# A hybrid decoder trunk: ten taps of the last depthwise-conv tile on GpSimd instead of TensorE

## The chip, the cores and the metric

The kernel runs on one core of one Trainium2 chip. The metric is device time in microseconds of one execution. Before the change the median of three runs is 987.44 us (986.02 to 987.93). A core has TensorE (PE, matrix products into PSUM; its weight loads are shown as PEld), VectorE (DVE), ScalarE (ACT), GpSimd (POOL) and SyncE (SP, which issues the DMAs). Each works through its own queue in order and waits on semaphores for the others.

## The reference

A trunk of two layers on 512 tokens of 1024 channels, in float32. The part that the change touches is in layer 0: a projection of the normed input gives, among others, the two halves of a gated unit of 512 channels. The gated result goes through a causal depthwise convolution of 31 taps, a LayerNorm over channels and a swish. Beside it runs a multi-head latent attention of 8 heads. Both results are joined and projected.

```
proj = h @ w_in
a, g = proj[..., :CONV_CH], proj[..., CONV_CH:c0]
u = a * jax.nn.sigmoid(g)
u = causal_dwconv(u, conv_w, conv_b)              # 31 taps, each channel by itself
u = jax.nn.silu(layernorm(u, conv_ln_g, conv_ln_b))
o = mla_attention(qn, qr, kn, kr, v)              # 8 heads, 128-query blocks, softmax
return jnp.concatenate([u, o], axis=-1) @ w_out
```

Then come a gated MLP with a 3-tap convolution (2816 wide), a pooling mixer and a second MLP in layer 1, and a final norm.

## The kernel before

Channels lie on the 128 partitions and the 512 tokens along the free dimension. Every projection is done as three products of rounded halves (`mm3`, L107 to L110: high by high, high by low, low by high), for which ScalarE rounds each weight tile (`split`, L97) and VectorE subtracts the rounded part from the raw one (L98; both of its inputs are in SBUF). `split_scaled` (L102, L103) does the same to activations with a factor per channel. SyncE streams the weights through three buffers.

The first RMSNorm: ScalarE squares the input tiles (L224), GpSimd adds the squares (L226), TensorE sums over channels (L239), VectorE forms the reciprocal root (L205 to L212), TensorE spreads it over rows (L261) and ScalarE copies it (L265). The gated unit (`glu`, L430 to L438) multiplies with these rows.

The convolution works on four tiles of 128 channels. For tiles 0 to 2, ScalarE opens an accumulator in PSUM, the bank `conv`, with the last tap and the bias (L382). VectorE then adds 30 taps, one `scalar_tensor_tensor` on 128x512 each (L399: `u` shifted by j, times the weight column, plus the accumulator), and ScalarE copies the accumulator to an SBUF tile `side` (L414). There is one bank `conv`, so a tile must be closed before the next one is opened. Tile 3 is different: its first ten taps are matrix products. For each, GpSimd scales the identity by the tap's weights (L391, 128x128) and TensorE multiplies that diagonal with the shifted `u` (L392) into another bank, `aux`. VectorE adds taps 10 to 30 to it, and ScalarE closes it with the bias.

The taps are background work. `conv` puts VectorE's taps of all tiles in one list, and `pump` emits a few of them at fixed places: three after each projection of a latent, three after each projection of a gated unit, and two after each of the four query blocks of a head (`BLK`). GpSimd's and TensorE's share of tile 3 is a second list, emitted on every other query block (`i % 2`). What is left is emitted after the last head. The framework then orders each engine's queue at build time by priority and by its own estimate of when operands are ready. Its order may differ from that of the source: taps of tile 3 that the source emits after all heads run among them.

Per head, TensorE makes the scores (L523), VectorE adds the mask and takes the maximum (L526: scores in PSUM, mask in SBUF), then forms the product of maximum and scale for two blocks at once (L533, 128x2, both inputs in SBUF). ScalarE takes the exponential (L537) and, after VectorE's reciprocal (L542), divides (L544). TensorE transposes (L558), ScalarE copies (L560), TensorE multiplies with the values (L571), and VectorE scales the queries of a later head (L512: PSUM and SBUF).

After the heads, TensorE transposes the four `side` tiles (L643), VectorE takes the LayerNorm statistics (L645, L646, then the root), VectorE and ScalarE normalize (L663, L669), TensorE transposes back (L680) and ScalarE applies the swish (L682). Between these TensorE works on the attention's share of the output projection; the convolution's share follows.

Of the kernel before, what the change touches and what calls it, by code (L numbers as in the profile page):

```python
# [8 lines left out]
F32 = mybir.dt.float32  # L9
F32R = mybir.dt.float32r  # L10
I32 = mybir.dt.int32
AF = mybir.ActivationFunctionType
ALU = mybir.AluOpType
AX = mybir.AxisListType

P = 128
S = 512
# [5 lines left out]
CW = 31  # L23
# [9 lines left out]
C_NE, C_CB, C_LG, C_LB, C_QG, C_KG, C_NO, C_PS, C_NF, C_FN = 0, 8, 12, 16, 20, 23, 25, 33, 41, 57  # L33
# [3 lines left out]
N_COL = C_FB + 2 * NF  # L37

WARM = 40
PE_TAPS = 10  # L40
W_PAD, T_PAD, R_PAD = 48, 16, 120
GLU, LAT, BLK, END = 3, 4, 2, 0

# [2 lines left out]
def kernel(  # L46
# [20 lines left out]
    act, dve, pool, pe = nc.scalar, nc.vector, nc.gpsimd, nc.tensor  # L67
# [11 lines left out]
    def uid(s):  # L79
        count[0] += 1  # L80
        return f"{s}{count[0]}"

    def bank():
        return p_ps.tile([P, S], F32, tag="ps", name=uid("ps"))

    def aux(tag="aux"):
        return p_ps.tile([P, S], F32, tag=tag, bufs=1, name=uid(tag))

    def temp():
        return p_t.tile([P, 2 + S], F32, tag="t", name=uid("t"))[:, :S]  # L90

    def small(n=4, dt=F32):
        return p_s.tile([P, 8], dt, tag=f"s{dt}", name=uid("s"))[:, :n]
# [70 lines left out]
    def weights(ahead=1):  # L164
        given[0] += 1
        while len(ready) < min(given[0] + ahead, len(stream)):
            prepare()
        w = ready[given[0] - 1]
        ready[given[0] - 1] = None
        return w  # L170
# [18 lines left out]
    def c(i):  # L189
        return col[:, i : i + 1]  # L190

    sq = p_c.tile([P, 3, P], F32, name="sq")
    ident, ones, fold_kr = sq[:, 0, :], sq[:, 1, :], sq[:, 2, :]
# [80 lines left out]
    p_m = tc.alloc_tile_pool(name="mixer", bufs=1, side="left", reuse_waits="tile")  # L274
# [79 lines left out]
    for k in range(KD):  # L354
        w = weights(2)
# [13 lines left out]

    u, ys, work, pe_work = [], [], [], []

    def conv(m):
        cw = C_CW + CW * m
        side = p_m.tile([P, S], F32, tag="side", bufs=4, name=uid("side"))
        ys.append(side)
        st = {}

        def open_acc():  # L380
            st["acc"] = aux("conv")
            act.activation(  # L382
                st["acc"], u[m][:, CW - 1 : CW - 1 + S], AF.Identity,
                bias=c(C_CB + m), scale=c(cw + CW - 1),
            )

        def pe_tap(j):
            if j == 0:
                st["acc"] = aux()
            d = p_m.tile([P, P], F32, tag="tapped", bufs=4, name=uid("tap"))  # L390
            pool.tensor_scalar(d, ident, c(cw + j), None, op0=ALU.mult)  # L391
            pe.matmul(st["acc"], d, u[m][:, j : j + S], start=j == 0, stop=j == PE_TAPS - 1)  # L392

        def tap(j):
            while m == 3 and pe_work:
                pe_work.pop(0)()
            if not st:
                open_acc()
            i = dve.scalar_tensor_tensor(  # L399
                st["acc"], u[m][:, j : j + S], c(cw + j), st["acc"],  # L400
                op0=ALU.mult, op1=ALU.add,
            )
            if held:
                tc.add_manual_dep(
                    i.ins, held.pop().ins.name,
                    mybir.DependencyInfo(
                        mybir.DependencyClass.NoSync, mybir.DependencyReason.DATA
                    ),
                    reason="background",
                )  # L410

        def close():
            bias = c(C_CB + m) if m == 3 else 0.0
            act.activation(side, st["acc"], AF.Identity, bias=bias, scale=1.0)  # L414

        n_pe = PE_TAPS if m == 3 else 0
        pe_work.extend((lambda j=j: pe_tap(j)) for j in range(n_pe))
        work.extend((lambda j=j: tap(j)) for j in range(n_pe, CW if m == 3 else CW - 1))
        work.append(close)

    def pump(nd, np_=0):
        for _ in range(min(np_, len(pe_work))):
            pe_work.pop(0)()
        for _ in range(min(nd, len(work))):
            work.pop(0)()


    def glu(ps_a, ps_g):
        t = temp()
        dve.tensor_tensor(t, ps_g, rows0, op=ALU.mult)  # L430
        s = temp()
        act.activation(s, t, AF.Sigmoid)
        if len(u) == 3:
            act.activation(spare, s[:, 0:1], AF.Exp)
        dve.tensor_tensor(s, s, rows0, op=ALU.mult)
        ut = p_m.tile([P, 640], F32, tag="u", bufs=4, name=uid("u"))[:, : CW - 1 + S]
        pool.memset(ut[:, : CW - 1], 0.0)
        dve.tensor_tensor(ut[:, CW - 1 :], ps_a, s, op=ALU.mult)  # L438
        u.append(ut)
        conv(len(u) - 1)  # L440
# [6 lines left out]
    def latent(n, gain, width):  # L447
        parts, stat = [], Squares(width, dve)
        for m in range(n):
            ps = project()  # L450
            parts.append(s4())
            split_scaled(pair(parts[m]), ps, c(gain + m))
            stat.add(ps)
            pump(LAT)
        return parts, stat
# [5 lines left out]
    for m in range(2):  # L461
        kv_ps.append(project())
        stat_kv.add(kv_ps[m])
        pump(LAT)
# [10 lines left out]
    for m in range(2):  # L475
        t = temp()
# [5 lines left out]
    for _ in range(2):  # L482
        ps_a = project()
        pump(GLU)
        ps_g = project()
        glu(ps_a, ps_g)
        pump(GLU)
# [27 lines left out]
    def scores(h):  # L515
        q, key = qs.pop(h), keys[h // 2 % 2][:, h % 2, :]
        pb = p_a.tile([P, 1280], F32, tag="prob", bufs=3, name=uid("prob"))
        mx, nb, ls = small(), small(), small()
        blocks, at = [], 0
        for i in range(4):  # L520
            w = (i + 1) * P
            ps = bank()
            pe.matmul(ps[:, :w], q[:, i * P : (i + 1) * P], key[:, :w], start=True, stop=True)  # L523
            p = pb[:, at : at + w]
            at += w
            dve.tensor_tensor_reduce(  # L526
                out=p, in0=ps[:, :w], in1=causal[:, S - w :], scale=1.0,
                scalar=-3.0e38, op0=ALU.add, op1=ALU.max, accum_out=mx[:, i : i + 1],
            )
            blocks.append(p)  # L530
            if i % 2:
                two = slice(i - 1, i + 1)
                dve.scalar_tensor_tensor(  # L533
                    nb[:, two], mx[:, two], -1.0, q_scale[:, two], op0=ALU.mult, op1=ALU.mult
                )
                for n in (i - 1, i):
                    act.activation(  # L537
                        blocks[n], blocks[n], AF.Exp, bias=nb[:, n : n + 1],
                        scale=q_scale[:, n : n + 1], accum_out=ls[:, n : n + 1],
                    )  # L540
            pump(BLK, i % 2)
        dve.reciprocal(ls, ls)  # L542
        for i in range(4):
            act.activation(blocks[i], blocks[i], AF.Copy, scale=ls[:, i : i + 1])  # L544
        probs[h] = blocks
        sums[h] = ls[:, 3:4]
# [56 lines left out]
    for h in range(HEADS):  # L603
        scores(h)
        if h % 2 == 0 and h + 2 < HEADS:
            keys_of(h // 2 + 1)
        if h >= 1:
            transposes(h - 1)
        if h + 2 < HEADS:
            queries(h + 2)  # L610
        if h >= 3 and h % 2:
            values(h - 3)
            values(h - 2)
        pump(END)
# [25 lines left out]
    for i in range(4):  # L640
# [3 lines left out]
        st = p_s.tile([P, 6], F32, tag="bn", bufs=2, name=uid("bn"))  # L644
# [12 lines left out]
    with tc.high_priority():  # L657
# [4 lines left out]
        for i in range(2):  # L662
            dve.tensor_scalar(  # L663
                yts[i], yts[i], mv[:, i, 0:1], r_ln[:, i : i + 1],
                op0=ALU.subtract, op1=ALU.mult,
# [9 lines left out]
    for m in range(4):  # L675
# [5 lines left out]
        t = temp()  # L681
# [181 lines left out]
    for h in range(2):  # L863
        w = weights()
        for i in range(4):
# [11 lines left out]
            if (h, i) >= (0, 2):  # L877
                while zps:
                    i, ps = zps.pop(0)
# [151 lines left out]
```

## Time and profile before

| | |
|---|---|
| median of three runs | 987.44 us |
| the profiled execution | 985.52 us |
| its span, first to last instruction | 983.8 us |
| mean granted TensorE clock | 0.995 |
| attention and conv taps together | about 101.7 to 183.5 us |
| L399, taps, bank `conv` | 90, 751 ns mean |
| L399, taps, bank `aux` | 21, 751 ns mean |
| L391, GpSimd's scaled diagonals | 10, 809 ns mean |

All times of instructions are from one profiled execution. A row of instructions has start, length, engine, line, operation, output, inputs and shapes, and a count where neighbours are merged; idle time before it and what ended that stand in square brackets. A row of a group has its count, total busy time and mean length. A row of waits has who waited for whom, the total in us, how often, and the longest. In the chain of waits, every piece of time is put down to the work that the next step needed. Neighbours on one engine overlap a little, since the next one starts while the last one drains, so distances between starts are often shorter than lengths.

### The profile page before, as it was taken

The page shows a single profiled execution, that of the slowest core. Times are in us where ns is not written, and L with a number is a line of the kernel's source. Part 1 is how long each engine was busy: PE and PEld are TensorE (multiplying, and loading weights), DVE is VectorE, ACT ScalarE, POOL GpSimd, SP SyncE. Part 2 cuts the span into 40 slices and gives each one's busy share as a digit, 9 for nine tenths or more (in the row PEclk, how much of TensorE's full clock was granted, in tenths as well). Part 3 has the DMA queues.
Part 4 walks back from the last instruction along what each step waited for, and adds up shares of the span by engine and source line. Part 5 has one row for each costly group of instructions (what it writes and reads, how often), then busy time and mean ns, then how long its engine had stood idle before and what let it go on. Part 6 is the DMA issues. An engine that isn't in the chain of part 4 may idle for free.

```text
span 983.8 us, 11537 instructions
## 1 busy us (share of the span) xinstructions
PE 966.6 (98%) x4464; PEld 795.2 (81%) x4464; DVE 582.5 (59%) x910; ACT 403.4 (41%) x590; POOL 70.4 (7%) x105
## 2 busy tenths in 40 slices
PE   8999999999999999999999999999999999999996
PEld 6888765788888888888888889888888888888886
DVE  5999989863765556565333348485656555532323
ACT  6435788362443433343222246253333334332321
POOL 6001100031000000000000103100000000000111
PEclk9999999999999999999999999999999999999998
DMA  6332110222232232223232341322222222323212
GB/s 231 118 123 81 39 43 1 87 86 88 80 111 93 100 105 89 98 94 108 86 107 86 107 139 44 108 91 103 88 105 101 93 93 101 104 89 107 86 43 86
DMA packets 29478, 91.99 MB, mean 94 GB/s; under 512 B 4080, under 2 KB 6384, under 8 KB 29424
## 3 DMA queue, kind: packets, MB, share of 16 engines
q1 hardware_dynamic: 28880, 90.74, 27.1%
q8 instruction: 35, 0.57, 0.2%
q10 hardware_dynamic: 544, 0.52, 0.2%
q14 instruction: 19, 0.16, 0.0%
HBM read 89.02 MB, written 2.23 MB: 93 GB/s over the span
## 4 chain that ended last, share of the span: by engine, by line
PE 95%; DVE 2%; DMA 1%; ACT 1%; SPq 0%; issue 0%; DVEq 0%
PE ps L108 29%; PE ps L109 29%; PE ps L110 29%; PE ps L571 2%; PE ps L523 1%; PE aux L392 1%; PE aux L239 1%; PE ps L558 1%; PE aux L261 1%; DMA col<-in_cols_dram 0%; DMA x<-in_xT_dram 0%; DVE conv L399 0%; PE ps L900 0%; PE ps L899 0%; ACT hi L97 0%
## 5 line engine op out<-in xcount | busy, mean ns | idle before, releaser
L97 ACT CAST hi<-raw 128x1024 fp32r<-128x1024 f32 (+2 forms) x166 | 169.9, 1025 | 372.1 <-PE ps L109 335.3
L108 PE MATMUL ps<-xgh,hi 128*128 128x512 f32 x816 | 319.2, 391 | 2.8 <-ACT hi L97 2.8
L109 PE MATMUL ps<-xgl,hi 128*128 128x512 f32 x816 | 317.9, 390 | 0.0
L110 PE MATMUL ps<-xgh,lo 128*128 128x512 f32 x816 | 317.3, 390 | 0.0
L98 DVE TENSOR_TENSOR lo<-raw,hi 128x1024 fp32r<-128x1024 f32 (+2 forms) x166 | 200.8, 1211 | 160.2 <-ACT hi L97 159.8
L108 PEld LDWEIGHTS ps<-xgh,hi 128*128 128x128 f32 x816 | 153.3, 188 | 35.0 <-ACT hi L97 3.8
L110 PEld LDWEIGHTS ps<-xgh,lo 128*128 128x128 f32 x816 | 153.1, 188 | 32.4 <-DVE lo L98 0.5
L109 PEld LDWEIGHTS ps<-xgl,hi 128*128 128x128 f32 x816 | 153.3, 188 | 31.3
L108 PE MATMUL ps<-gh,hi 128*128 128x512 f32 (+1 forms) x374 | 141.2, 378 | 0.0
L109 PE MATMUL ps<-gl,hi 128*128 128x512 f32 (+1 forms) x374 | 141.1, 377 | 0.0
L110 PE MATMUL ps<-gh,lo 128*128 128x512 f32 (+1 forms) x374 | 141.0, 377 | 0.0
L108 PEld LDWEIGHTS ps<-gh,hi 128*128 128x128 f32 x374 | 70.4, 188 | 12.9
L109 PEld LDWEIGHTS ps<-gl,hi 128*128 128x128 f32 x374 | 70.4, 188 | 12.9
L110 PEld LDWEIGHTS ps<-gh,lo 128*128 128x128 f32 x374 | 70.4, 188 | 12.9
L728 DVE TENSOR_TENSOR t<-ps,rows 128x512 f32<-128x512 f32 x44 | 30.4, 691 | 77.2 <-PE ps L110 77.2
L226 POOL TENSOR_TENSOR sqr<-sqr,sqr 128x512 f32<-128x512 f32 x33 | 50.2, 1521 | 311.9 <-ACT sqr L224 282.0
L740 DVE TENSOR_TENSOR t<-ps,rows 128x512 f32<-128x512 f32 x44 | 30.4, 691 | 67.0 <-PE ps L110 66.8
L399 DVE SCALAR_TENSOR_TENSOR conv<-u,col,conv 128x512 f32<-128x512 f32 x90 | 67.6, 751 | 1.0 <-ACT conv L382 0.5
L735 DVE SCALAR_TENSOR_TENSOR t<-t,col,t 128x512 f32<-128x512 f32 x88 | 65.7, 749 | 1.4
L738 ACT ACTIVATE t<-t 128x512 f32<-128x512 f32 x44 | 27.8, 631 | 74.7 <-DVE t L735 74.7
L108 PE MATMUL ps<-s,hi 128*128 128x512 f32 x96 | 39.4, 419 | 0.0
L727 POOL MEMSET t<- 128x2 f32 x44 | 4.2, 99 | 491.1 <-DVE t L741 350.3
(187 smaller groups left out, 832.4 us busy)
## 6 DMA issues: line engine op xcount, KB each, us to landing
raw<-in_w_up_dram SPq DMA_DIRECT2D x88, 512.0 KB, 3.2
raw<-in_w_down_dram SPq DMA_DIRECT2D x44, 512.0 KB, 3.2
raw<-in_w_in_dram SPq DMA_DIRECT2D x10, 512.0 KB, 3.2
raw<-in_w_out_dram SPq DMA_DIRECT2D x8, 512.0 KB, 3.2
x<-in_xT_dram SPq DMA_DIRECT2D x8, 256.0 KB, 4.1
raw<-in_w_in_dram SPq DMA_DIRECT2D x8, 256.0 KB, 3.7
raw<-in_w_uq_dram SPq DMA_DIRECT2D x4, 384.0 KB, 3.0
raw<-in_w_ukv_dram SPq DMA_DIRECT2D x2, 512.0 KB, 4.1
```

The lines of the kernel that those rows point to most:

```text
L97: i = act.copy(dst[0], src)
L98: dve.tensor_tensor(dst[1], src, dst[0].bitcast(F32), op=ALU.subtract)
L108: pe.matmul(ps, a[0], b[0], start=start, stop=False)
L109: pe.matmul(ps, a[0], b[1], start=False, stop=False)
L110: pe.matmul(ps, a[1], b[0], start=False, stop=stop)
L226: self.engine.tensor_tensor(self.parts[0], self.parts[0], t, op=ALU.add)
L399: i = dve.scalar_tensor_tensor(st["acc"], u[m][:, j : j + S], c(cw + j), st["acc"], op0=ALU.mult, op1=ALU.add,)
L571: pe.matmul(ps[:, j * P :], vals[j][:, e, hp * P : (hp + 1) * P], pt, start=e == 0 and j == 0, stop=e == 1 and j == 3,)
L728: dve.tensor_tensor(ut[:, 2 : 2 + S], pu, rows, op=ALU.mult)
L735: dve.scalar_tensor_tensor(a, ut[:, j : j + S], c(fw + j * NF + f), a, op0=ALU.mult, op1=ALU.add)
L738: act.activation(a, a, AF.Silu)
L740: dve.tensor_tensor(b, pv, rows, op=ALU.mult)
```

## The change

The ten products of tile 3 on TensorE, and the ten scaled diagonals, go. Instead GpSimd computes taps 0 to 9 itself: a multiplication of the shifted `u` by the weight column, broadcast along the tokens, into a tile (for tap 0 into `side` itself), and for taps 1 to 9 an addition into `side`, 19 instructions on 128x512. Tile 3 now opens in the bank `conv` like the others, with the last tap and the bias on ScalarE, and VectorE adds taps 10 to 29. The close of tile 3 is an addition on VectorE of the accumulator and `side`, instead of ScalarE's copy. The temporary tiles become two of 128x512 instead of four of 128x128. GpSimd's list is emitted one tap per query block instead of one per two.

```diff
-PE_TAPS = 10
+POOL_TAPS = (0, 0, 0, 10)
...
-        def pe_tap(j):
-            if j == 0:
-                st["acc"] = aux()
-            d = p_m.tile([P, P], F32, tag="tapped", bufs=4, name=uid("tap"))
-            pool.tensor_scalar(d, ident, c(cw + j), None, op0=ALU.mult)
-            pe.matmul(st["acc"], d, u[m][:, j : j + S], start=j == 0, stop=j == PE_TAPS - 1)
+        def pool_tap(j):
+            t = side
+            if j:
+                t = p_m.tile([P, S], F32, tag="tapped", bufs=2, name=uid("tapped"))
+            w = c(cw + j).to_broadcast([P, S])
+            pool.tensor_tensor(t, u[m][:, j : j + S], w, op=ALU.mult)
+            if j:
+                pool.tensor_tensor(side, side, t, op=ALU.add)
 
         def tap(j):
-            while m == 3 and pe_work:
-                pe_work.pop(0)()
             if not st:
                 open_acc()
...
         def close():
-            bias = c(C_CB + m) if m == 3 else 0.0
-            act.activation(side, st["acc"], AF.Identity, bias=bias, scale=1.0)
-
-        n_pe = PE_TAPS if m == 3 else 0
-        pe_work.extend((lambda j=j: pe_tap(j)) for j in range(n_pe))
-        work.extend((lambda j=j: tap(j)) for j in range(n_pe, CW if m == 3 else CW - 1))
+            if n_pool:
+                dve.tensor_tensor(side, st["acc"], side, op=ALU.add)
+            else:
+                act.copy(side, st["acc"])
+
+        n_pool = POOL_TAPS[m]
+        pool_work.extend((lambda j=j: pool_tap(j)) for j in range(n_pool))
+        work.extend((lambda j=j: tap(j)) for j in range(n_pool, CW - 1))
         work.append(close)
...
-            pump(BLK, i % 2)
+            pump(BLK, 1)
```

More of the change, by code (lines that the diff above doesn't have):

```diff
@@ L368, in project @@
         return ps
-    u, ys, work, pe_work = [], [], [], []
+    u, ys, work, pool_work = [], [], [], []
     def conv(m):
@@ L412, in close @@
         def close():
-            bias = c(C_CB + m) if m == 3 else 0.0
-            act.activation(side, st["acc"], AF.Identity, bias=bias, scale=1.0)
-        n_pe = PE_TAPS if m == 3 else 0
-        pe_work.extend((lambda j=j: pe_tap(j)) for j in range(n_pe))
-        work.extend((lambda j=j: tap(j)) for j in range(n_pe, CW if m == 3 else CW - 1))
+            if n_pool:
[5 more added lines that the diff above has]
+        work.extend((lambda j=j: tap(j)) for j in range(n_pool, CW - 1))
         work.append(close)
     def pump(nd, np_=0):
-        for _ in range(min(np_, len(pe_work))):
-            pe_work.pop(0)()
+        for _ in range(min(np_, len(pool_work))):
+            pool_work.pop(0)()
         for _ in range(min(nd, len(work))):
```

## The prediction

> **What bounds the kernel now.** I read the busy totals and the chain of waits of the page first, then the stretches of time around the changed tile, then who waited for whom there, and last the single instructions on VectorE (DVE), GpSimd (POOL), ScalarE (ACT) and TensorE (PE).
>
> ```profile
> PE 966.6 (98%) x4464; PEld 795.2 (81%) x4464; DVE 582.5 (59%) x910; ACT 403.4 (41%) x590; POOL 70.4 (7%) x105
> PE 95%; DVE 2%; DMA 1%; ACT 1%; SPq 0%; issue 0%; DVEq 0%
> ```
>
> Over the whole span TensorE is the bound, and work taken from its queue seems to be worth its full length. That average hides the stage that the change touches. The columns below are stretch, length, then busy time and instructions of PE, PEld, DVE, ACT and POOL, the granted clock and the DMA.
>
> ```profile
> core 0: us, PE busy (x) PEld busy (x) DVE busy (x) ACT busy (x) POOL busy (x), PEclk, DMA share, GB/s
> 88.00:101.70 13.70, 13.70 (x60) 10.97 (x59) 11.43 (x16) 10.50 (x19) 0.14 (x1) 1.00 0.28 96
> 101.70:141.50 39.80, 39.80 (x165) 26.96 (x164) 35.83 (x91) 30.61 (x74) 4.33 (x6) 1.00 0.12 41
> 141.50:183.50 42.00, 39.54 (x179) 27.78 (x178) 40.66 (x86) 29.02 (x69) 0.00 (x0) 1.00 0.08 26
> 183.50:195.00 11.50, 9.91 (x50) 7.51 (x49) 9.35 (x27) 6.06 (x9) 0.00 (x0) 1.00 0.27 91
> ```
>
> From 101.7 to 183.5 us (attention, with the conv taps between) VectorE is busy 35.83 + 40.66 = 76.5 of 81.8 us. Only 5.3 us are idle, most of it for these reasons:
>
> ```profile
> DVE q L512 <- PE ps L110: 2.5, 3, 2.0
> DVE prob L526 <- PE ps L523: 1.3, 3, 0.5
> DVE conv L399 <- ACT conv L382: 0.5, 1, 0.5
> ```
>
> So VectorE is a second bound. The last conv tile can't end before VectorE has done its share, and what follows needs that end:
>
> ```profile
> 174.74 8.67 DVE L399 SCALAR_TENSOR_TENSOR aux<-u,col,aux 128x512 f32<-128x512 f32 x11
> 183.91 0.69 ACT L414 ACTIVATE side<-aux,col 128x512 f32<-128x512 f32 x1
> 184.65 0.66 PE L643 MATMUL aux<-sq,side 128*128 128x128 f32 x4
> 194.89 0.33 PE L680 MATMUL aux<-sq,t 128*128 128x128 f32 x1 [1.59 <-ACT t L669]
> ```
>
> The last tap ends at 174.74 + 8.67 = 183.41, ScalarE closes the tile, TensorE transposes it, the LayerNorm statistics follow, and at 194.89 TensorE itself has run dry and waits 1.59 us for the result. Both chains end within 1.6 us of each other. A gain needs both to get shorter; a delay of the conv chain alone is paid in full once it passes this point.
>
> **What is removed.**
>
> ```profile
> L392 PE MATMUL aux<-u,tap x20: 592/593/594, 102.4 to 139.3; 128*128 128x512 f32 x20
> 102.53 0.86 PE aux L392 x2
> 139.03 0.86 PE aux L392 x2
> ```
>
> Each of the ten diagonal products is two passes and takes 0.86 us of the chain (first and last are shown), 8.6 us in all. If TensorE were the only bound, the time would fall by 8.6. It isn't: the same taps have left VectorE in both versions. VectorE has 21 taps of tile 3 now (10 to 30). After, it has 20 (10 to 29; the last goes to an opening on ScalarE as for other tiles) and one addition in the close. Such a tensor-tensor instruction on a PSUM and an SBUF operand costs about what a tap does, so I put this at nothing. What VectorE can win is its waits for TensorE, 2.5 + 1.3 = 3.8 us. I take -3.0, bounds -3.8 and 0.
>
> Also removed are the ten scalings of the identity on GpSimd. Four of them sit early, between the sums of squares of the first RMSNorm:
>
> ```profile
> 18.35 3.70 POOL L391 TENSOR_SCALAR tap<-sq,col 128x128 f32<-128x128 f32 x4
> 22.02 2.98 POOL L226 TENSOR_TENSOR sqr<-sqr,sqr 128x512 f32<-128x512 f32 x2
> 25.20 0.95 PE L239 MATMUL aux<-sq,sqr 128*128 128x2 f32 x8
> 31.59 1.25 PE L261 MATMUL aux<-d,sq 128*128 128x128 f32 x8
> 32.87 0.59 ACT L265 COPY rows<-aux 128x512 f32<-128x512 f32 x1 [0.27 <-PE aux L261]
> 33.78 1.28 DVE L430 TENSOR_TENSOR t<-ps,rows 128x512 f32<-128x512 f32 x2
> ```
>
> The sums can end 3.70 us earlier. TensorE doesn't stall there, but the row factors at 32.87 release the first GLU at 33.78, which opens VectorE's tap chain. The projections that GLU also needs end at about the L261 row, 31.59 us, so at most some 1.9 us come off. I take -1.0, bounds -1.9 and 0, since the queue's new order isn't known.
>
> **What is added on GpSimd.** Nineteen instructions on 128x512: ten multiplications by a broadcast column, nine additions into `side`. They can start when the fourth GLU output is there:
>
> ```profile
> 95.43 0.68 DVE L438 TENSOR_TENSOR u<-ps,t 128x512 f32<-128x512 f32 x1
> L226 POOL TENSOR_TENSOR sqr<-sqr,sqr x33: 1264/1619/2149, 10.4 to 957.6; 128x512 f32<-128x512 f32 x33
> ```
>
> At 1.26 to 1.62 us each they last 24 to 31 us, from 96 to about 120 to 127. The broadcast multiplication has no row; even at four times a 128-column scaling of 0.9 us (3.70 over four) it would end before 150. `side` is wanted at about 183, so GpSimd's own time is hidden with 30 us or more to spare. Nothing else is queued on GpSimd in that time.
>
> What isn't hidden is what its reads do to VectorE. Three rows of GpSimd's additions beside VectorE's splits and residuals show it:
>
> ```profile
> 212.07 1.79 POOL L226 TENSOR_TENSOR sqr<-sqr,sqr 128x512 f32<-128x512 f32 x1 [2.54 <-ACT sqr L224]
> 211.96 0.75 DVE L103 SCALAR_TENSOR_TENSOR xgl<-x,col,xgh 128x512 fp32r<-128x512 f32 x1
> 212.62 1.79 DVE L103 SCALAR_TENSOR_TENSOR xgl<-x,col,xgh 128x512 fp32r<-128x512 f32 x1
> 213.93 1.62 POOL L226 TENSOR_TENSOR sqr<-sqr,sqr 128x512 f32<-128x512 f32 x1
> 214.72 1.37 DVE L695 TENSOR_TENSOR x<-ps,x 128x512 f32<-128x512 f32 x2 [0.31 <-PE ps L110]
> ```
>
> The second split (two tensors in SBUF) took 1.79 instead of 0.75: it sat until GpSimd's addition ended at 213.86 and then ran. The residual that reads PSUM and one SBUF tensor was not touched: two in 1.37 us, the first wholly under an addition. So taps (`u` in SBUF, accumulator in PSUM) are safe, and instructions with two SBUF tensors are not. In GpSimd's stretch (window 96 to 126 us) those are:
>
> ```profile
> 96.03 0.95 DVE L98 TENSOR_TENSOR lo<-raw,hi 128x768 fp32r<-128x768 f32 x1
> L98 DVE TENSOR_TENSOR lo<-raw,hi 128x768 fp32r<-128x768 f32 x3 | 2.9, 952 | 0.0
> L533 DVE SCALAR_TENSOR_TENSOR s<-s,misc 128x2 f32<-128x2 f32 x6 | 0.9, 152 | 0.0
> ```
>
> One of the three splits begins as the GLU output lands, at 96.03, so two count, and the six 128x2 products of maximum and scale. A tiny instruction beside a reading GpSimd has no row here. Its loss lies between nothing and the 1.04 us of the split's row. A hit lands on average in the middle of an addition of some 1.4 us, and GpSimd is nearly always busy then: 0.65 us. I treat the tiny ones like the split, the nearest row, since that one waited for the lock and not for bandwidth: 8 x 0.65 = +5.2. Bounds: two splits alone 1.3, all eight at 1.04 8.3. VectorE executes in order, so each wait delays all taps and scores queued behind it.
>
> The Trainium skill (SBUF — State Buffer, section "Who interferes with whom") gives this as a rule: a VectorE instruction with two SBUF inputs and a GpSimd instruction that reads SBUF lock each other out for a whole instruction, whatever the size. The L103 row agrees. By the rule the sum below stands at +2.4; by the lower bound, which spares tiny instructions, it would be -1.5.
>
> **What is moved.** Tile 3 loses its own accumulator: it was in the bank `aux`, and now waits for the bank `conv` until tile 2 has closed.
>
> ```profile
> 141.55 0.75 DVE L399 SCALAR_TENSOR_TENSOR aux<-u,col,aux 128x512 f32<-128x512 f32 x1
> 96.89 4.71 DVE L399 SCALAR_TENSOR_TENSOR conv<-u,col,conv 128x512 f32<-128x512 f32 x6
> 165.23 0.75 DVE L399 SCALAR_TENSOR_TENSOR aux<-u,col,aux 128x512 f32<-128x512 f32 x1
> 165.88 0.75 DVE L399 SCALAR_TENSOR_TENSOR conv<-u,col,conv 128x512 f32<-128x512 f32 x1
> L414 ACT ACTIVATE side<-conv x3: 579/601/633, 88.4 to 171.9; 128x512 f32<-128x512 f32 x3
> L382 ACT ACTIVATE conv<-u,col x3: 765/784/793, 36.9 to 132.2; 128x512 f32<-128x512 f32 x3
> ```
>
> Taps on one accumulator run 4.71 / 6 = 0.785 apart; alternating between the two, 0.65. Some 16 taps alternate, the first at 141.55 and the last before 171 us, which is worth up to 2.1 us; other work can stand between them, so +1.0, bounds 0 and 2.1. The turn of the bank is a close of 0.60 and an opening of 0.78 on ScalarE, in which VectorE has no tap: +0.8, bounds 0 and 2 (the 0.5 idle above is such a turn, partly covered). At the end the close is VectorE's own addition: the 1.24 us from 183.41 to 184.65 shrink to a hand-over, -1.1, bounds -0.6 and -1.1.
>
> TensorE, 8.6 us ahead, will idle in this stage. A short idle already costs clock:
>
> ```profile
> 196.00:199.00 3.00, 2.98 (x13) 2.42 (x13) 0.80 (x2) 2.89 (x5) 0.10 (x1) 0.50 0.56 175
> ```
>
> After the 1.59 us wait the granted clock was 0.50. Another 3.4 us at that rate would cost 1.7; I take +0.5, bounds 0 and 1.7.
>
> **The sum**, in us: -3.0 (waits for TensorE) -1.0 (earlier statistics) +5.2 (port) +1.0 (one accumulator) +0.8 (turn of the bank) -1.1 (close) +0.5 (clock) = +2.4. The profiled execution took 985.52, 1.92 below the median of 987.44. So the change makes 987.9 of the one and 989.8 of the other; I forecast the median, 989.8.
>
> **The rivals.** First, the small instructions slip past GpSimd: only two splits wait (1.3 in place of 5.2, -3.9), and the scheduler covers the single accumulator and the turn of the bank (-1.8). The sum is then -3.3, 984.1 us, faster. For it: no row shows a tiny instruction blocked, and TensorE gives up 8.6 us. Against it: the split waited for the whole addition. It decides when VectorE loses less than about 2.6 us in all at the port (-1.8 and +2.4 - 5.2 + 2.6 make -2.0). Chance 0.23.
>
> Second, the terms cancel: half of the tiny ones' loss, +5.2 becoming 2.6, gives -0.2, 987.2 us. For it: the waits that VectorE loses at GpSimd's port may partly fall where it waited for TensorE anyway. Chance 0.27.
>
> Third, TensorE's clock. If the idle time spreads over two more stretches of 3.4 us that delay the transposes, 2 x 1.7 replaces the 0.5: 989.8 + 2.9 = 992.7 us. For it is the 0.50 row; against it, that most of the idle time lies where TensorE's speed isn't the bound. Chance 0.10. The Trainium skill (TensorE: Matmul & The Clock Gate, Part 1) asks for an idle window of about 3.4 us before the clock halves; here a wait of 1.59 us, with short gaps before it, preceded the halving.
>
> **How the numbers follow.** My forecast has 0.40; its own range is 989 to 993. Slower by over 0.2% (2 us, about what a measurement of this kernel can tell from no change) holds the forecast and the clock rival, 0.50. Faster is the first rival, 0.23, the same is the second, 0.27. The range runs from 984.5, which leaves out the faster half of the first rival, to 994.5, which takes in nearly three more blocked instructions at 0.65 above the third rival's price.
>
> **What would show it.** Right: no L392 on TensorE, 19 GpSimd instructions ending before 150 us, L533 means well over 0.152 us in GpSimd's stretch, VectorE without waits for TensorE there, the last tap at or after 183.4, and a longer TensorE wait before L680. Wrong: L533 still at 0.15 us, the last tap some 4 us earlier, and L680 earlier than 194.9 with the same wait.

## The result and the profile after

The kernel became slower: 992.16 us (median of four runs, 991.9 to 993.04) against 987.4 (four runs, 986.02 to 987.93), ratio 1.0051 [1.0039, 1.0063]. That is about 5 us more, where +2.4 was forecast. The profiled execution took 991.9 us, its span is 990.1 and its mean granted clock 0.988. The profiled execution before is 1.9 us below its own median and this one 0.3, so the two traces lie further apart (6.3 us in span) than the medians. Below, a ratio is turned into us by 987.4; an interval of ±0.1% is ±1 us, and the difference of two such ratios is known to about 1.3 to 1.7 us.

First the busy totals and the shares of the chain of waits from the page of the changed kernel.

```profile
PE 964.5 (97%) x4444; PEld 793.6 (80%) x4444; DVE 587.9 (59%) x910; ACT 404.1 (41%) x590; POOL 85.3 (9%) x114
PE 92%; DVE 4%; ACT 1%; issue 1%; DMA 1%; POOL 0%; SPq 0%; DVEq 0%
```

The twenty passes have left TensorE (4464 to 4444), yet it is busy only 2.1 us less, and its share of the chain fell from 95 to 92% while VectorE's doubled. Part of what TensorE gave up came back as waiting for VectorE. The stretches around the changed tile show where (stretch, length, busy time and instructions by engine, granted clock, DMA):

```profile
core 0: us, PE busy (x) PEld busy (x) DVE busy (x) ACT busy (x) POOL busy (x), PEclk, DMA share, GB/s
101.70:141.50 39.80, 38.30 (x169) 26.69 (x169) 38.26 (x91) 33.12 (x82) 19.61 (x17) 1.00 0.14 44
141.50:183.50 42.00, 38.86 (x167) 27.19 (x166) 39.88 (x82) 29.10 (x67) 0.00 (x0) 0.96 0.08 26
183.50:195.00 11.50, 8.87 (x43) 6.87 (x41) 10.65 (x15) 4.18 (x6) 0.00 (x0) 1.00 0.37 103
```

TensorE has more idle time in all three than before. VectorE is busy 78.1 of 81.8 us in the first two, 1.6 more than before, and 10.65 of 11.5 us in the third. Its remaining waits from 101.7 to 183.5 us (who for whom, total, count, longest) are these:

```profile
DVE prob L528 <- PE ps L525: 1.1, 2, 0.6
DVE conv L399 <- ACT conv L382: 0.6, 1, 0.6
DVE s L98 <- ACT s L97: 0.2, 1, 0.2
```

The 3.8 us of waits for TensorE shrank to 1.1. GpSimd's nineteen instructions (shortest, median and longest in ns, first and last start, then the last one) and what its reads do to VectorE from 96 to 130 us (busy us, mean ns, then single rows) follow.

```profile
L392 POOL TENSOR_TENSOR tapped<-u,col x9: 1027/1037/1042, 100.4 to 119.3; 128x512 f32<-128x512 f32 x9
120.43 1.27 POOL L394 TENSOR_TENSOR side<-side,tapped 128x512 f32<-128x512 f32 x1
L535 DVE SCALAR_TENSOR_TENSOR s<-s,misc 128x2 f32<-128x2 f32 x7 | 4.2, 603 | 0.0
L98 DVE TENSOR_TENSOR lo<-raw,hi 128x768 fp32r<-128x768 f32 x3 | 3.4, 1138 | 0.0
106.35 0.66 DVE L535 SCALAR_TENSOR_TENSOR s<-s,misc 128x2 f32<-128x2 f32 x1
106.95 3.25 POOL L394 TENSOR_TENSOR side<-side,tapped 128x512 f32<-128x512 f32 x2
107.55 1.52 DVE L98 TENSOR_TENSOR lo<-raw,hi 128x768 fp32r<-128x768 f32 x1
108.99 1.24 DVE L535 SCALAR_TENSOR_TENSOR s<-s,misc 128x2 f32<-128x2 f32 x1
114.26 0.53 DVE L535 SCALAR_TENSOR_TENSOR s<-s,misc 128x2 f32<-128x2 f32 x1
117.12 0.91 DVE L535 SCALAR_TENSOR_TENSOR s<-s,misc 128x2 f32<-128x2 f32 x1
121.15 0.58 DVE L535 SCALAR_TENSOR_TENSOR s<-s,misc 128x2 f32<-128x2 f32 x1
```

GpSimd ended at 121.7, far ahead of the close. The products of maximum and scale, 128x2, took 603 ns on average instead of 152, and one took 1.24 us; the three splits took 1138 ns instead of 952. Together 7 x 0.45 + 3 x 0.19 = 3.7 us of VectorE's time. The single rows show that this falls on six instructions: five products and one split began while GpSimd was at work (98.7 to 121.7 us) and lost 0.38 to 1.09 us each, 0.62 on average; the other two products and two splits lost nothing. By the rule of the Trainium skill (SBUF — State Buffer, section "Who interferes with whom") the size of the blocked instruction doesn't matter; the 1.24 us of an instruction on two columns agrees.

Now single rows around the stage's beginning and end: GpSimd's additions and VectorE's splits beside them in the first RMSNorm, TensorE's wait there, the first and the fourth GLU, the last taps, the close, and the first transpose behind the statistics.

```profile
15.56 6.85 POOL L226 TENSOR_TENSOR sqr<-sqr,sqr 128x512 f32<-128x512 f32 x4
17.81 3.46 DVE L103 SCALAR_TENSOR_TENSOR xgl<-x,col,xgh 128x512 fp32r<-128x512 f32 x2
23.01 0.74 PE L110 MATMUL ps<-xgh,lo 128*128 128x512 f32 x2 [0.46 <-DVE lo L98]
36.29 1.28 DVE L432 TENSOR_TENSOR t<-ps,rows 128x512 f32<-128x512 f32 x2
97.95 0.68 DVE L440 TENSOR_TENSOR u<-ps,t 128x512 f32<-128x512 f32 x1
172.06 11.05 DVE L399 SCALAR_TENSOR_TENSOR conv<-u,col,conv 128x512 f32<-128x512 f32 x14 [0.62 <-ACT conv L382]
191.24 0.69 DVE L414 TENSOR_TENSOR side<-conv,side 128x512 f32<-128x512 f32 x1
200.50 1.14 PE L682 MATMUL aux<-sq,t 128*128 128x128 f32 x4 [4.46 <-DVE t L665]
```

The first additions of GpSimd in that norm, before and in the changed kernel:

```profile
10.45 7.93 POOL L226 TENSOR_TENSOR sqr<-sqr,sqr 128x512 f32<-128x512 f32 x5 [8.26 <-ACT sqr L224]
11.11 11.30 POOL L226 TENSOR_TENSOR sqr<-sqr,sqr 128x512 f32<-128x512 f32 x7 [8.93 <-ACT sqr L224]
```

The first GLU opens 2.51 us later than before (36.29 for 33.78), the fourth GLU output is 2.52 later (97.95 for 95.43), and the stage from there to the first L682 lasts 102.55 us instead of 99.46: 3.1 more. Of the 2.51 us, 0.66 is there already when GpSimd's first addition starts, ahead of the place where the scalings stood (11.11 for 10.45): that much is no effect of the change at this place, and 1.85 come behind it. TensorE waits 4.46 us there instead of 1.59. All of tile 3's VectorE taps stand in the tail, on one accumulator: 14 of the 20 follow each other in 11.05 us, 0.79 apart. After L682 the two traces differ by 0.7 us more (span 6.3 in all, 2.5 + 3.1 + 0.7).

So there are two losses: a start that was meant to be earlier and is later, and a stage that is longer. The experiments take them apart.

### The profile page after: what moved, and what is told of

It is laid out like the page before. It is cut to its first block, busy times and chain, and to the rows that moved or that the text cites. A ratio compares the mean times of both kernels' runs of the same rounds, so it can differ in the third digit from the quotient of the medians.

```text
span 990.1 us, 11510 instructions
## 1 busy us (share of the span) xinstructions
PE 964.5 (97%) x4444; PEld 793.6 (80%) x4444; DVE 587.9 (59%) x910; ACT 404.1 (41%) x590; POOL 85.3 (9%) x114
## 4 chain that ended last, share of the span: by engine, by line
PE 92%; DVE 4%; ACT 1%; issue 1%; DMA 1%; POOL 0%; SPq 0%; DVEq 0%
PE ps L108 29%; PE ps L110 29%; PE ps L109 29%; PE ps L573 1%; DVE conv L399 1%; PE ps L560 1%; DVE lo L98 1%; PE aux L239 1%; DVE prob L528 1%; PE aux L261 1%; DMA x<-in_xT_dram 1%; PE ps L525 0%; POOL sqr L226 0%; PE ps L902 0%; PE ps L901 0%
## 5 line engine op out<-in xcount | busy, mean ns | idle before, releaser
L399 DVE SCALAR_TENSOR_TENSOR conv<-u,col,conv 128x512 f32<-128x512 f32 x110 | 82.6, 751 | 1.8 <-ACT conv L382 0.6
```

Source lines behind the costliest of these rows:

```text
L399: i = dve.scalar_tensor_tensor(st["acc"], u[m][:, j : j + S], c(cw + j), st["acc"], op0=ALU.mult, op1=ALU.add,)
```

## The experiments

My theory after the result: (A) without the four early scalings the start gets later, because GpSimd's additions run unbroken and block VectorE's splits, for which TensorE waits; (B) in the stage, GpSimd's reads and the one accumulator cost more than TensorE's relief gives. The rivals: the later start is chance, and the whole loss of the stage is GpSimd's reads.

**The start.** In the kernel before, all ten scalings wait behind GpSimd's last clearing of `v`; nothing else is changed.

```diff
-            pool.tensor_scalar(d, ident, c(cw + j), None, op0=ALU.mult)
+            with tc.issue_after(v_clear.ins):
+                pool.tensor_scalar(d, ident, c(cw + j), None, op0=ALU.mult)
...
-        pool.memset(v, 0.0)
+        v_clear = pool.memset(v, 0.0)
```

> The kernel before, with GpSimd's ten scalings of the identity queued behind the last clearing of v, so that none of them stands between the squares of the first RMSNorm. Nothing else changes. If VectorE's splits at the start lose time to GpSimd's uninterrupted additions (in the changed kernel three of them took about 1.77 us where 0.75 is the length alone), the first GLU comes about 2 us later and the time rises by 1.5 to 2.5 us over the kernel before, to about 989 to 990. If the late start of the changed kernel was the chance of one profile (its first additions began 0.66 us later on account of a DMA), the time stays within 0.5 us of before.

Measured: 989.17 us, ratio 1.0018 [1.0009, 1.0027], so +1.8 us. Its rows at the start, the first statistics product and the first GLU:

```profile
15.10 6.82 POOL L226 TENSOR_TENSOR sqr<-sqr,sqr 128x512 f32<-128x512 f32 x4
17.32 3.47 DVE L103 SCALAR_TENSOR_TENSOR xgl<-x,col,xgh 128x512 fp32r<-128x512 f32 x2
22.52 0.73 PE L110 MATMUL ps<-xgh,lo 128*128 128x512 f32 x2 [1.54 <-DVE lo L98]
27.20 0.95 PE L239 MATMUL aux<-sq,sqr 128*128 128x2 f32 x8
35.76 1.28 DVE L431 TENSOR_TENSOR t<-ps,rows 128x512 f32<-128x512 f32 x2
```

Four additions run back to back, VectorE's two splits take 3.47 us beside them, and TensorE then stands 1.54 us in the brackets of the third row, waiting for a split. In the kernel before, the scalings stand in the middle of this:

```profile
17.15 2.55 DVE L103 SCALAR_TENSOR_TENSOR xgl<-x,col,xgh 128x512 fp32r<-128x512 f32 x2
```

Both are done 2.55 us after the first one's start instead of 3.47, and TensorE doesn't wait for a split there. GpSimd's sums end earlier without the scalings, as I had said (21.92 in place of 25.00 us), but the statistics product L239 that reads them comes later (27.20 in place of 25.20): TensorE's queue has the same 72 passes ahead of it, and those wait for the splits. The same wait for `lo` stands in all six traces without the four scalings (1.5 to 1.6 us in four of them; 0.5 in two where TensorE was slower just then, the changed kernel's among them with a granted clock of 0.75 from 16 to 20 us), and in none of those with them.

The counterpart: in the changed kernel, four scalings of the identity into tiles that nobody reads stand where four of the ten had stood.

```diff
+        def spare_scaling(j):
+            d = p_m.tile([P, P], F32, tag="unread", bufs=4, name=uid("unread"))
+            pool.tensor_scalar(d, ident, c(cw + j), None, op0=ALU.mult)
...
+        pool_work.extend((lambda j=j: spare_scaling(j)) for j in range(4 if n_pool else 0))
...
-            pump(BLK, 1)
+            pump(BLK, 5 if pool_work and len(pool_work) > 10 else 1)
```

> The changed kernel, with four scalings of the identity on GpSimd that nobody reads, at the place between the squares of the first RMSNorm where the kernel before had them. If the lock at the start is a part of the loss, this added work makes the changed kernel faster by 1.5 to 2.5 us, to about 990. If the start was chance, it stays at 992.

Measured: 990.52 us, 1.003 [1.0019, 1.0042], about 2 us less than the changed kernel, with the first GLU at 34.73. A holds both ways; what is left, +3.0, is the stage's.

**GpSimd's load alone.** The kernel before with the nineteen instructions added, into tiles that nobody reads; TensorE keeps its products.

```diff
+        def load(j):
+            t = unread
+            if j:
+                t = p_m.tile([P, S], F32, tag="load", bufs=1, name=uid("load"))
+            w = c(cw + j).to_broadcast([P, S])
+            pool.tensor_tensor(t, u[m][:, j : j + S], w, op=ALU.mult)
+            if j:
+                pool.tensor_tensor(unread, unread, t, op=ALU.add)
...
+            if loads:
+                loads.pop(0)()
             pump(BLK, i % 2)
```

> The kernel before, ten products on TensorE included, plus the nineteen GpSimd instructions of the change on tiles that nobody reads. GpSimd's load alone is added; VectorE's, ScalarE's and TensorE's work stays. If GpSimd's reads cost VectorE 3 to 4 us between 96 and 125 us and VectorE's chain sets the end, the time rises by about 2 to 4 us, to 989.5 to 991.5. If TensorE is the bound there and VectorE's waits have room, it stays within 1 us of before.

Measured: 990.79 us, 1.0031 [1.0019, 1.0044], +3.1 us. VectorE's rows from 96 to 130 us:

```profile
L545 DVE SCALAR_TENSOR_TENSOR s<-s,misc 128x2 f32<-128x2 f32 x6 | 4.3, 714 | 0.0
L98 DVE TENSOR_TENSOR lo<-raw,hi 128x768 fp32r<-128x768 f32 x3 | 3.2, 1057 | 0.0
```

The loss there is 6 x 0.56 + 3 x 0.11 = 3.7 us, and the time is longer by nearly as much, which fits that on this kernel VectorE's loss beside GpSimd's reads is paid almost in full. It isn't the only effect: GpSimd's later scalings now stand between the added instructions, and TensorE waits 0.9 us for one of them.

**The bank.** The changed kernel, with tile 3 opened in the bank `aux`, as it was before.

```diff
-            st["acc"] = aux("conv")
+            st["acc"] = aux("aux" if m == 3 else "conv")
```

> The changed kernel, with tile 3 opened in the bank aux in place of conv, so that its taps can alternate with those of tile 2 again and need not wait for the turn of the bank. If the shared bank costs 1 to 3 us (taps 0.785 apart instead of 0.66, and the turn), the time falls to 989 to 991. If only GpSimd's lock and the start matter, it stays at 992.

Measured: 986.6 us, 0.9992 [0.9983, 1.0001]. That takes back 5.8 us (0.59%). Its products of maximum and scale (96 to 130 us), two taps in the tail, the close, and the first transpose after the statistics:

```profile
L535 DVE SCALAR_TENSOR_TENSOR s<-s,misc 128x2 f32<-128x2 f32 x8 | 3.6, 448 | 0.0
172.44 0.75 DVE L399 SCALAR_TENSOR_TENSOR aux<-u,col,aux 128x512 f32<-128x512 f32 x1
173.10 0.75 DVE L399 SCALAR_TENSOR_TENSOR conv<-u,col,conv 128x512 f32<-128x512 f32 x1
182.94 0.69 DVE L414 TENSOR_TENSOR side<-aux,side 128x512 f32<-128x512 f32 x1
195.54 1.00 PE L682 MATMUL aux<-sq,t 128*128 128x128 f32 x4 [0.83 <-ACT t L671]
```

The port still takes 8 x 0.30 = 2.4 us, but the taps alternate 0.66 apart, and the close stands at 182.94 instead of 191.24 (0.85 of these 8.3 us is an earlier fourth GLU output, 97.10 for 97.95). To see whether the order does this or the bank itself, the next kernel keeps two banks and forces the order of one: VectorE's first tap of tile 3 is queued behind the last tap of tile 2.

```diff
+            if m == 2:
+                last_of_2[:] = [i]
+            elif m == 3 and last_of_2:
+                tc.add_manual_dep(
+                    i.ins, last_of_2.pop().ins.name,
+                    mybir.DependencyInfo(
+                        mybir.DependencyClass.NoSync, mybir.DependencyReason.DATA
+                    ),
+                    reason="serial",
+                )
```

> The kernel of e4 (tile 3 in its own bank), with VectorE's first tap of tile 3 queued behind the last tap of tile 2. The bank is free, so no turn is waited for; only the taps can't alternate and tile 3's can't be drawn forward. If that order is what the shared bank cost, most of the 5.6 us between e4 and the changed kernel comes back: 990 to 992. If it was the turn of the bank (close and opening on ScalarE), it stays at 986.6 to 987.5.

Measured: 990.67 us, 1.0038 [1.0024, 1.0052]: 0.46%, 4.5 us, slower than with the own bank in free order. The tail and the close:

```profile
171.04 11.83 DVE L399 SCALAR_TENSOR_TENSOR aux<-u,col,aux 128x512 f32<-128x512 f32 x15
189.87 0.68 DVE L424 TENSOR_TENSOR side<-aux,side 128x512 f32<-128x512 f32 x1
```

So the order carries most of it; 1.3 us are left for the turn of the bank, a remainder that isn't told from zero. The order costs in two ways. The taps run 0.79 apart instead of 0.66. And VectorE's queue is laid out anew: the splits of weights (between 97 and 170 us, by line, with shapes) come ahead of the taps. First the changed kernel, then the one with its own bank:

```profile
L98 DVE TENSOR_TENSOR lo<-raw,hi x6: 945/1206/1519, 98.5 to 151.6; 128x768 fp32r<-128x768 f32 x3, 128x1024 fp32r<-128x1024 f32 x3
```

```profile
L98 DVE TENSOR_TENSOR lo<-raw,hi x4: 945/948/1221, 97.7 to 131.0; 128x768 fp32r<-128x768 f32 x3, 128x1024 fp32r<-128x1024 f32 x1
```

Three splits of 128x1024 instead of one, 2 x 1.22 us, stand before 170 us in the changed kernel, and as many in the forced one. They are not extra work: with its own bank the kernel does two such splits after the close, between the statistics. Counted up to the first transpose behind the statistics it has five of them ahead, the changed kernel and the forced one six, so 1.2 us of the 4.5 is work moved forward. The slower taps are an estimate: in the stage, 31 taps follow directly on a tap of the same accumulator in the forced order and 3 with the own bank in free order, and 28 x 0.13 makes 3.6 us. The two parts together come near the 4.5; no run prices them apart.

**TensorE's relief alone.** With the own bank, taps 0 to 9 of tile 3 are left out of the computation, and ScalarE closes the tile. Nobody does the ten taps.

```diff
-            if n_pool:
-                dve.tensor_tensor(side, st["acc"], side, op=ALU.add)
-            else:
-                act.copy(side, st["acc"])
+            act.copy(side, st["acc"])
...
-        pool_work.extend((lambda j=j: pool_tap(j)) for j in range(n_pool))
```

> The kernel of e4 (tile 3 in its own bank) with taps 0 to 9 of tile 3 left out altogether: neither TensorE nor GpSimd does them, and ScalarE closes the tile. It prices the relief of TensorE without GpSimd's load. If GpSimd's load costs what e3 showed (3.2 us), this comes at about 983.4, that is 3.2 below e4. If TensorE were the only bound and 8.6 us of it freed, it would come at about 979 to 980. If the load is hidden once the bank is its own, it stays at e4's 986.6.

Measured: 985.52 us, 0.9986 [0.9977, 0.9995]. A miss: I had expected more to come off. Against the kernel with late scalings (0.9986 for 1.0018) it is 3.2 us faster, with one tap less on VectorE as well; against the own bank with GpSimd's taps only 0.6, which can't be told from zero. Giving the ten taps to nobody is worth hardly more than giving them to GpSimd.

**The small instructions.** The product of maximum and scale as two instructions on one column, with the scale as a pointer scalar, so that only one operand is a tensor.

```diff
-                dve.scalar_tensor_tensor(
-                    nb[:, two], mx[:, two], -1.0, q_scale[:, two], op0=ALU.mult, op1=ALU.mult
-                )
+                for n in (i - 1, i):
+                    dve.tensor_scalar(
+                        nb[:, n : n + 1], mx[:, n : n + 1], q_scale[:, n : n + 1], -1.0,
+                        op0=ALU.mult, op1=ALU.mult,
+                    )
```

> The kernel of e4, with the product of maximum and scale formed by two tensor-scalar instructions on 128x1 (scale as a pointer scalar) in place of one scalar-tensor-tensor on 128x2, so that it has one SBUF tensor only. If the tiny products are what waits for GpSimd (five of them lost about 3.2 us together in the profile of the changed kernel), the time falls by 1.5 to 2.5 us to 984 to 985, since sixteen more short instructions cost about 1 us. If the waits are mostly the weight splits', it stays within 0.5 us of e4 or rises by 1.

Measured: 986.67 us, 0.9997 [0.9989, 1.0006], no gain. Its rows from 96 to 130 us:

```profile
L536 DVE TENSOR_SCALAR s<-s,misc 128x1 f32<-128x1 f32 x13 | 2.3, 205 | 0.0
L98 DVE TENSOR_TENSOR lo<-raw,hi 128x768 fp32r<-128x768 f32 x3 | 3.8, 1271 | 0.0
```

Two of the small ones take 0.41 us where one product took 0.45, and the splits wait longer (1271 ns for 947): what the small ones save, the splits lose. With the four unread scalings added to it (the condition in `pump` reads `len(pool_work) > POOL_TAPS[3]` from here on, which for ten taps is the same),

> The kernel of e6, with the four unread scalings of e2 at the start. If the three costs (start 1.5, bank 5.6, tiny products about 2) are separate, they add up and the time is 982.5 to 984, faster than both kernels. If the scalings' gain belongs to e2's order alone, it stays at e6's time.

it measured 985.2 us, 0.998 [0.9972, 0.9989]: 1.7 us better, again the start. With sixteen taps on GpSimd besides, in place of ten (`POOL_TAPS = (0, 0, 0, 16)`),

> The kernel of e7, with sixteen instead of ten taps of tile 3 on GpSimd: VectorE has six taps fewer (about 4 us), GpSimd works 14 us longer. If VectorE still bounds the stage, it falls by another 1 to 3 us, to 980 to 983. If TensorE has become the bound, it stays at e7's time.

it measured 985.42 us, 0.9982 [0.9971, 0.9992]: nothing more. The close and the first statistics:

```profile
179.49 0.69 DVE L418 TENSOR_TENSOR side<-aux,side 128x512 f32<-128x512 f32 x1
185.65 0.70 DVE L654 BATCH_NORM_STATS2 bn<-aux 128x6 f32<-128x512 f32 x1 [5.47 <-PE aux L652]
```

The close comes at 179.49, and VectorE then waits 5.47 us for TensorE's transposes. There the conv chain isn't the bound any more: six taps fewer on VectorE won nothing.

**The best version**: the changed kernel with the own bank and the four unread scalings, both edits shown above (with that condition in `pump`).

> The kernel of e4 with the four unread scalings of e2 at the start and the original product of maximum and scale. If the cost at the start adds up with the bank's, and the change of e6 was worth nothing, it comes at 985 to 985.3, like e7. If e7's time needed the tensor-scalar products, it stays near 986.6.

Measured: 984.85 us, 0.9975 [0.9965, 0.9985], 2.5 us faster than the kernel before and 7.5 faster than the changed one.

```profile
18.17 4.22 POOL L398 TENSOR_SCALAR unread<-sq,col 128x128 f32<-128x128 f32 x4
34.06 1.28 DVE L437 TENSOR_TENSOR t<-ps,rows 128x512 f32<-128x512 f32 x2
193.89 1.00 PE L687 MATMUL aux<-sq,t 128*128 128x128 f32 x4 [0.80 <-ACT t L676]
```

The first GLU is back near 34 us, and the first transpose after the statistics comes 6.6 us ahead of the changed kernel's. What TensorE waits for there is now ScalarE, 0.80 us.

## Why the prediction was right and wrong

The direction was right, and so was the reason: VectorE is a second bound in this stage, so TensorE's 8.6 us were not to be had, and what the change adds on VectorE's path outweighs the relief. The size was half of what was measured, +2.4 for +5.0. By the terms:

- **Earlier statistics, -1.0, bounds -1.9 and 0: the step that failed, in its sign.** It cost +1.8 to take the scalings out of the start alone, and about 2 was won when they were put back. This difference of 2.8 us is as large as the whole miss; without the term the sum is +3.4, and the kernel with its start restored measured +3.0. In the kernel before, the step had no way to gain: from the statistics product L239 to the first GLU it is 8.58 us before (25.20 to 33.78), 8.57 in the changed kernel and 8.56 with late scalings, and L239 (no wait in brackets) starts when TensorE's queue reaches it, not when the sums are done. I priced only what GpSimd's earlier sums could gain and looked at TensorE not waiting for them. What TensorE does wait for, once the scalings are gone, is VectorE's splits: the additions then follow each other without a gap, and each split waits one of them out. I had quoted that very lock and used it only for the later stage.
- **VectorE's waits for TensorE, -3.0, and the close, -1.1.** The waits fell by 2.7 in the trace. With nobody doing the ten taps, 3.2 us came off; one tap of VectorE, some 0.7, is part of that, so TensorE's relief was worth about 2.5 (an estimate). That kernel says nothing on the close, which is ScalarE's there as before. In the changed kernel's trace VectorE's addition ends at 191.93 and the first statistics start at 193.24, 1.31 us later; before, the last tap ended at 183.41 and they started at 185.35, 1.94 later. So 0.6 came off and not 1.1, since VectorE had a split of 1.23 us queued in between. Sixteen taps on GpSimd show the limit: TensorE's part of the stage is next.
- **Port, +5.2.** The mechanism held: tiny instructions are blocked like large ones. At 3.7 us, VectorE lost less than 8 x 0.65, because of the count: a blocked instruction lost 0.62 on average, but six were blocked and not eight. The prediction counted them to 126 us; GpSimd was done at 121.7, and the last split began at 124.12. What the load costs in time depends on the rest: +3.1 on the kernel before, but with an own bank and TensorE relieved +0.6, which can't be told from zero.
- **One accumulator, +1.0, and turn of the bank, +0.8, bounds together 0 to 4.1.** This was the term most wrong in size: with GpSimd's load present the two are worth 5.8, beyond the upper bound, and 4.5 of it is the order. The pitch that I used was right (0.79 and 0.66). What I left out is that all of tile 3's taps then stand in the tail, and that VectorE's splits are moved ahead of them.
- Port and bank together were put at 7.0 and are 6.4 (the changed kernel against the one without the ten taps, 1.0051 for 0.9986, a tap of VectorE included). That this agrees is partly luck: the two don't add. Each is paid only as far as the conv chain is the latest, and which of them gets the blame depends on which is removed first.
- **Clock, +0.5.** The granted clock was 0.50 from 196 to 203 us instead of to 199, and the traces differ by 0.7 us behind L682. Of the clock rival's further stretches one came in the stage, around a wait of TensorE of 2.88 us for ScalarE that ended at 161.59. It didn't delay the transposes, before which TensorE waited 4.46 us for VectorE, and the best version has such a stretch too (0.50 from 160 to 166 us) with the shortest time. The two stretches in the changed kernel:

```profile
162.00:164.00 2.00, 2.00 (x10) 1.67 (x10) 2.00 (x6) 2.00 (x6) 0.00 (x0) 0.50 0.00 0
196.00:203.00 7.00, 2.53 (x12) 1.92 (x12) 3.96 (x18) 2.73 (x4) 0.00 (x0) 0.50 0.00 1
```

Of the signs named in advance, all came: no L392 on TensorE, GpSimd done before 150 us, the small products above 0.152 us, VectorE's waits for TensorE nearly gone, a late last tap and a longer wait of TensorE. None of them looked at the start, where the sum was wrong. The first rival fell, since the small instructions did not slip past; the second, that terms cancel, holds only for the kernel with its own bank (0.9992). Its 2.6 is half of what all eight instructions were to lose; half of the six tiny ones alone is 2.0, and the sum would have been +0.4 in place of -0.2. The turn of the bank alone, and the load's price on a shared bank, were not tried.

## What to carry to other kernels

When work leaves the bound engine, count what each other engine has to do in that stage and on how many independent accumulators: a bank that is shared "like the others" forces an order, and here that order cost 4.5 us, where the port cost 0.6 to 3.1 depending on what else held up the stage. Look also at what the removed instructions stood between: four small GpSimd operations that looked like overhead let VectorE's splits through between longer ones, and the kernel without them is 1.8 us slower. Prices of two delays in one stage needn't add, as the port's and the bank's didn't; those in two stages did here (start 2.1 and bank 5.8, together 7.5). Try the pair, not only each by itself.

## What the hardware showed beyond that

- GpSimd's multiplication by a broadcast column takes 1.04 us on 128x512, less than the 1.28 us of its addition of two full tensors.

```profile
L394 POOL TENSOR_TENSOR side<-side,tapped x9: 1262/1282/1879, 102.3 to 120.4; 128x512 f32<-128x512 f32 x9
```

- The longest of these additions, 1.88 us, is one of the pair at 106.95, beside the 1.52 us split: the lock holds up GpSimd as well.
- A VectorE instruction on one column with a pointer scalar took 0.205 us on average from 96 to 130 us, under GpSimd's load, where one on two columns with two tensors took 0.45 to 0.71 in the same window of other runs.
- Half the clock from 196 to 203 us fell where TensorE was busy only 2.53 of the 7 us, and behind L682 the two traces are 0.7 us apart.
